# Two token roots by one product with a tile of ones and a power on 288 columns, and a final stage in two token halves: a decoder step on one core

## The chip, the core and the metric

The kernel runs on one core of a Trainium2 chip. The metric is the device time of one execution in microseconds. TensorE (PE in the profile) does the matrix products, VectorE (DVE) and ScalarE (ACT) the elementwise work, GpSimd (POOL) a few small operations, SyncE (SP) issues nearly all transfers.

## The reference

One step of a decoder with a single layer, in f32, for 256 prompt tokens and 8 x 4 sample tokens: 288 columns in all, 2048 features. Each of the nine sequences has its own conditioning vector, and so its own shift, scale and gate.

```python
def _rms(x, gain):
    y = xf * lax.rsqrt(jnp.mean(xf * xf, axis=-1, keepdims=True) + EPS)
    return y * gain

h = _rms(x, g_mix) * (1 + sc_m) + sh_m
proj = h @ w_in                       # seven parts, 9216 columns
...                                   # short convolution, gated MLP mixer, merge
x = x + gt_m * (merged @ w_out)
h2 = _rms(x, g_ffn) * (1 + sc_f) + sh_f
gate, up = jnp.split(h2 @ w_ffn_in, 2, axis=-1)
x = x + gt_f * ((silu(gate) * up) @ w_ffn_out)
y = _rms(x, g_final)
```

There are four means of squares: of x before `w_in` (the first root), of v inside the mixer, of x before `w_ffn_in` (the second root), and of the final x. Each gives one number for each token, mean to the power of -0.5, with which all features of that token are multiplied.

## The kernel before, in words

Features lie on the partitions, in 16 tiles of 128, and the 288 tokens on the columns. Every weight tile is loaded as f32 (`raw`) and split into a high part by a cast on ScalarE (L458) and a low part by a subtraction on VectorE (L464, in the first stage L249); the activations are split too. `triple` (L230, L233, L235) makes three products for each tile: high by high, high by low, low by high. The conditioning products (L401) are placed between the blocks.

TensorE's order is written out by hand: a list of steps, in which `later(f, gap)` puts a small piece of work behind so many further triples. In the first stage, up to `free`, the order of ScalarE, VectorE and SyncE is the program's order too; there `jobs` are run one at a time when a finished tile has been evicted. Afterwards a scheduler orders these engines. On each engine instructions run in their order, so one that waits holds up those behind it.

A root is made in four moves. The squares are summed over the 16 tiles on VectorE (`acc`, in the first stage `q`). `square_sum` (L204) takes 128 tokens at a time as weights and multiplies with one column of `ones`, which leaves the sums with the tokens on the partitions, 128 x 3. `roots` makes mean plus epsilon on VectorE (L217) and the power on GpSimd (L218), with a tile of -0.5 as exponent. `rstd_bcast` (L225) spreads the three columns back over all partitions by three transpositions.

First root: `sums1` and `norm1` are put behind 12 and 8 triples in the block `wA[2]`. `norm1` copies the result to `rb` on ScalarE (L622); `normed` (L309) multiplies x with it, and from there h1 is made (low parts in L657), which `wA[4]` needs. Before that the products run on x that is not yet normed (`xe`), and are put right later.

Second root: `rstd2` puts the sums 9 triples into the block `fk[0]`, the transpositions (`norm2`) 7 triples later, the copy is L931. The four blocks `fk` run on x without the norm (`xg`); the blocks `fi` behind them need h2 = `normed` (L309), scaled and shifted (L318, L321, L322) and split (L323, L328).

The final stage: the last residual (L345 for the prompt tokens, L351 and L354 for the sample tokens), its square (L173), the sums, one root for all tokens, and `finish` multiplies x by the spread root in nine pieces of one or two feature tiles (L986), each stored at once (L987). `warm` (L581) runs idle products in the waits.

Of the kernel before, what the change touches and what calls it, by code (L numbers as in the profile page):

```python
# [24 lines left out]
RAW = 7  # L25
# [6 lines left out]
EPS = 1e-6  # L32
# [21 lines left out]
TB = (0, 128, 160)  # L54
# [47 lines left out]
def _body(tc, nc, d, pc, pw, pslot, ptmp, pps):  # L102
    ids = [0]

    def nm(s):
        ids[0] += 1
        return f"{s}_{ids[0]}"

    def const(name, shape, dt=F32):
        return pc.tile(shape, dt, tag=name, name=name)  # L110

    def slot(dt=F32, shape=(P, T)):
        return pslot.tile(list(shape), dt, tag="s", name=nm("s"), padded_shape=[P, TU])
# [28 lines left out]
    x = const("x", [P, 16, T])  # L142
# [5 lines left out]
    ones = const("ones", [P, P])  # L148
    V.memset(ones, 1.0)
    mhalf = const("mhalf", [P, 16])  # L150
# [7 lines left out]
    mod = const("mod", [P, 96, NC])  # L158
# [7 lines left out]
    class SquareSum:  # L166
        def __init__(self):
            self.acc, self.last = None, None

        def add(self, a, cuts=((0, T),)):  # L170
            q = tmp() if self.last is not None else ptmp.tile([P, T], F32, tag="acc", name=nm("acc"), bufs=1)
            for o, e in cuts:
                A.activation(q[:, o:e], a[:, o:e], AF.Square)  # L173
            if self.last is not None:
                if self.acc is None:
                    self.acc = self.last
                else:
                    V.tensor_tensor(self.acc, self.acc, self.last, ALU.add)  # L178
            self.last = q

    def token_rstd(ss, n, half=False, gaps=None):
        got = {}
        V.tensor_tensor(ss.acc, ss.acc, ss.last, ALU.add)

        def fold():
            got["ps"] = psmisc()
            square_sum(got["ps"], ss.acc, True, True)

        steps = [fold, lambda: roots(got, n, half)]
        for f, gap in zip(steps, gaps or (0, 0, 0)):  # L190
            if gaps:
                later(f, gap)
            else:
                f()
        return got

    def sums(got, ss, first):
        if first:
            got["ps"] = psmisc()
        square_sum(got["ps"], ss.acc if first else ss.last, first, not first)  # L200

    def square_sum(ps, a, first, last):
        for tb, o in enumerate(TB):
            PE.matmul(  # L204
                ps[:, tb : tb + 1],
                a[:, o : o + 128],
                ones[:, 0:1],
                start=first and tb == 0,
                stop=last,
                skip_group_check=True,  # L210
            )

    def roots(got, n, half):
        ps = got["ps"]
        r = got["r"] = ptmp.tile([P, 3], F32, tag="r", name=nm("r"), bufs=2)
        e = ptmp.tile([P, 3], F32, tag="e", name=nm("e"), bufs=2)
        V.tensor_scalar(e, ps[:, 0:3], 1.0 / n, EPS, ALU.mult, ALU.add)  # L217
        G.tensor_tensor(r, e, mhalf[:, 0:3], ALU.pow)  # L218
        if half:
            V.tensor_scalar(r, r, 0.5, None, ALU.mult)  # L220

    def rstd_bcast(got):
        r, ps = got["r"], psmisc()
        for tb, o in enumerate(TB):
            PE.transpose(ps[:, o : o + P], r[:, tb : tb + 1].to_broadcast([P, P]), ident)  # L225
        return ps[:, :T]

    def triple(out, w, a, first, last, turn=False):
        (wh, wl), (ah, al) = w, a
# [46 lines left out]
    def later(f, gap=0):  # L276
        if not pending:
            since[0] = 0
        pending.append((f, gap))
# [27 lines left out]
    def normed(kt, rb):  # L307
        t = slot()
        V.tensor_tensor(t, x[:, kt, :], rb, ALU.mult)  # L309
        return t  # L310
# [27 lines left out]
            if i >= 2:  # L338
                finish_(ks[i - 2])

    def residual(m, ps, gt0, prompt_first=False):
        t = tmp()

        def prompt():
            V.scalar_tensor_tensor(  # L345
                x[:, m, :TP], ps[:, :TP], mod[:, gt0 + m, 0:1], x[:, m, :TP], ALU.mult, ALU.add
            )

        if prompt_first:
            prompt()  # L350
        V.tensor_tensor(sam(t[:, TP:]), sam(ps[:, TP:T]), bc4(mod[:, gt0 + m, 1:]), ALU.mult)  # L351
        if not prompt_first:
            prompt()
        V.tensor_tensor(x[:, m, TP:], t[:, TP:], x[:, m, TP:], ALU.add)  # L354

    def gelu2(a):
# [8 lines left out]
    class Step:  # L365
        defer = False
        raw = None
        parts = None

    class Ada(Step):  # L370
# [17 lines left out]
        half = None  # L388
# [183 lines left out]
    S = {}  # L572
# [5 lines left out]
    def warm(n, out=None):  # L578
        out = idle if out is None else out
        for _ in range(n):  # L580
            PE.matmul(out[:, :T], wb[:, :P], wb, start=True, stop=True)  # L581
# [30 lines left out]
        }  # L612

    def sums1():
        got = S["r1"] = {"ps": psmisc()}
        square_sum(got["ps"], S.pop("sq"), True, True)
        roots(got, D, False)

    def norm1():
        ps = rstd_bcast(S["r1"])  # L620
        S["rb1"] = ptmp.tile([P, T], F32, tag="rb", name=nm("rb"), bufs=1)
        A.copy(S["rb1"], ps)  # L622

        make_h1(0, 2)

    made = {}
# [144 lines left out]
    def sinkD(m, ps):  # L771
        a = part[m]
        V.tensor_tensor(a, ps[:, :T], a, ALU.add)  # L773
        if 32 <= m < 40:
            gelu2(a)
            if m == 32:
                S["accv"] = SquareSum()
            S["accv"].add(a)
        elif 24 <= m < 32:
            gelu2(a)  # L780
            u2[m - 24] = a
        elif m >= 40:
            A.activation(a, a, AF.Tanh, scale=0.5)
        elif m >= 16:
            mix_conv(m - 16)
# [22 lines left out]
            SY.dma_start(d["o_z"], zout)  # L808

    def v_stats():  # L810
        S["rv"] = token_rstd(S["accv"], 4096, True, (2, 0))
# [111 lines left out]
    h2, xg = {}, {}  # L923

    def rstd2():
        S["r2"] = token_rstd(S["acc2"], D, gaps=(9, 0))

    def norm2():
        ps = rstd_bcast(S["r2"])
        S["rb2"] = ptmp.tile([P, T], F32, tag="rb", name=nm("rb"), bufs=1)  # L930
        A.copy(S["rb2"], ps)  # L931
# [30 lines left out]

    def sink_fo(q):
        def f(m, ps):
            ending = q == 3 and m == 15
            residual(m, ps, 80, ending)
            if q == 3:
                if m == 0:
                    S["acc3"] = SquareSum()
                S["acc3"].add(x[:, m, :], ((0, TP), (TP, T)) if ending else ((0, T),))  # L970
                A.activation(x[:, m, :], x[:, m, :], AF.Copy, scale=gfin[:, m : m + 1])

        return f

    def finish():
        got, acc, keep = {}, S["acc3"], psmain()
        sums(got, acc, True)
        warm(5, keep)
        sums(got, acc, False)
        warm(10, keep)  # L980
        roots(got, D, False)
        rb = rstd_bcast(got)
        cuts = (0, 1, 2, 4, 6, 8, 10, 12, 14, 16)
        for i, j in zip(cuts, cuts[1:]):
            v = x[:, i:j, :]
            V.tensor_tensor(v, v, rb.unsqueeze(1).to_broadcast([P, j - i, T]), ALU.mult)  # L986
            SY.dma_start(d["o_y"][:, i:j, :], v)  # L987


    rh1 = h1.__getitem__  # L990
# [28 lines left out]
    steps = [Do(lambda: warm(24)), a0[0], Do(lambda: warm(5)), a0[1]]  # L1019
# [50 lines left out]
    n = len(steps)  # L1070
# [30 lines left out]
    for s in steps:  # L1101
# [11 lines left out]
        i = pos[id(s)]  # L1113
# [119 lines left out]
```

## Time and profile before

| | |
|---|---|
| median of 3 runs | 1627.19 us (1626.94 to 1627.59) |
| the profiled execution | 1627.47 us |
| its span | 1625.7 us |
| TensorE products, weight loads | 1614.2, 1550.0 us busy |
| VectorE, ScalarE, GpSimd | 1016.5, 736.1, 20.8 us busy |
| moved by transfers | 357.60 MB |

The span is the profiled time from the first instruction to the last; the rest of the execution's time lies around it. In a row of the timeline stand start, duration, engine, line, operation, what is written and read, and in brackets the engine's idle time before and what ended it. Rows of several instructions have one start and their whole duration. The chain of work that ended last is followed back from the last instruction; its rows have start, length, engine, tile and line.

### The profile page before, as it was taken

What the parts mean: (1) busy time and instruction counts of PE and PEld (TensorE: products, weight loads), DVE (VectorE), ACT (ScalarE), POOL (GpSimd) and SP (SyncE); (2) the same over time, 40 slices, a digit from 0 to 9 for tenths busy, and PEclk for the clock granted to TensorE, in tenths of its full rate; (3) what the DMA queues carried; (4) which work ended last, traced back from release to release, by engine and by line L of the source; (5) the groups of instructions that cost most, each with busy time, mean ns of one, the idle gap of its engine ahead of it and who ended that gap; (6) DMA issues with size and microseconds to landing.
All of it is one profiled execution on the core that took longest, in us unless ns stands there. A gap on an engine that the chain in (4) does not pass through costs nothing.

```text
span 1625.7 us, 31608 instructions
## 1 busy us (share of the span) xinstructions
PE 1614.2 (99%) x12649; PEld 1550.0 (95%) x12649; DVE 1016.5 (63%) x2196; ACT 736.1 (45%) x1357; POOL 20.8 (1%) x65
## 2 busy tenths in 40 slices
PE   9999999999999999999999999999999999999997
PEld 8998999999999999999999999999999999999997
DVE  6676788877755567667744555555555555555565
ACT  5633344643444334456633444444444444344453
POOL 0000000000000000011000000000000000000000
PEclk9999999999999999999999999999999999999999
DMA  9887866777777666654576556453464534644341
GB/s 374 325 319 276 318 232 212 281 275 295 294 296 310 260 258 225 245 175 160 186 303 263 210 179 207 157 173 110 169 222 156 175 114 161 225 159 171 113 156 59
DMA packets 59428, 357.60 MB, mean 220 GB/s; under 512 B 6768, under 2 KB 9872, under 8 KB 28560
## 3 DMA queue, kind: packets, MB, share of 16 engines
q1 hardware_dynamic: 58992, 355.45, 59.8%
q8 instruction: 99, 1.62, 0.4%
q14 instruction: 49, 0.40, 0.1%
q10 hardware_dynamic: 288, 0.13, 0.0%
HBM read 352.46 MB, written 3.09 MB: 219 GB/s over the span
## 4 chain that ended last, share of the span: by engine, by line
PE 98%; DMA 1%; DVE 0%; issue 0%; SPq 0%; DVEq 0%; ACT 0%
PE pm L230 31%; PE pm L233 30%; PE pm L235 30%; PE ada L401 5%; DMA raw<-in_a 1%; DVE x L986 0%; PE px L204 0%; PE px L233 0%; PE px L230 0%; PE px L825 0%; PE px L235 0%; PE px L866 0%; PE pm L581 0%; PE px L867 0%; PE px L868 0%; PE px L225 0%
## 5 line engine op out<-in xcount | busy, mean ns | idle before, releaser
L230 PE MATMUL pm<-s,hi 128*128 128x288 f32 (+1 forms) x3750 | 1109.0, 296 | 0.0
L233 PE MATMUL pm<-s,hi 128*128 128x288 f32 (+1 forms) x3750 | 1105.0, 295 | 0.0
L235 PE MATMUL pm<-s,lo 128*128 128x288 f32 (+1 forms) x3738 | 1101.2, 295 | 0.0
L458 ACT CAST hi<-raw 128x512 fp32r<-128x512 f32 (+1 forms) x963 | 587.2, 612 | 809.3 <-PE pm L233 780.1
L464 DVE TENSOR_TENSOR lo<-raw,hi 128x512 fp32r<-128x512 f32 (+1 forms) x849 | 577.6, 682 | 438.8 <-ACT hi L458 426.3
L230 PEld LDWEIGHTS pm<-s,hi 128*128 128x128 f32 x3750 | 705.1, 188 | 15.2 <-issue 13.3
L233 PEld LDWEIGHTS pm<-s,hi 128*128 128x128 f32 x3750 | 704.7, 188 | 0.0
L235 PEld LDWEIGHTS pm<-s,lo 128*128 128x128 f32 x3738 | 702.7, 188 | 0.0
L249 DVE TENSOR_TENSOR lo<-raw,hi 128x512 fp32r<-128x512 f32 x111 | 74.6, 675 | 28.9 <-ACT hi L458 28.2
L401 PE MATMUL ada<-raw,cs 128*32 128x512 f32 (+2 forms) x1152 | 88.2, 452 | 0.7 <-DMA raw<-in_a 0.6
L401 PEld LDWEIGHTS ada<-raw,cs 128*32 128x32 f32 x1152 | 30.8, 110 | 45.7 <-issue 41.4
L773 DVE TENSOR_TENSOR s<-pm,s 128x288 f32<-128x288 f32 x72 | 32.8, 456 | 19.8 <-PE pm L235 19.8
L345 DVE SCALAR_TENSOR_TENSOR x<-pm,mod,x 128x256 f32<-128x256 f32 x80 | 38.0, 475 | 2.7 <-PE pm L235 2.7
L304 DVE TENSOR_TENSOR s<-t,s 128x288 fp32r<-128x288 f32 (+1 forms) x76 | 34.5, 458 | 6.4 <-ACT s L302 6.4
L302 ACT CAST s<-t 128x288 fp32r<-128x288 f32 (+1 forms) x76 | 32.5, 432 | 12.9 <-DVE t L805 12.4
L951 DVE SCALAR_TENSOR_TENSOR t<-t,pm 128x288 f32<-128x288 f32 x42 | 19.1, 454 | 20.6 <-PE pm L235 20.6
L765 DVE TENSOR_TENSOR s<-pm,s 128x288 f32<-128x288 f32 x48 | 21.8, 454 | 10.6 <-PE pm L235 9.5
L351 DVE TENSOR_TENSOR t<-pm,mod 128x32 f32<-128x32 f32 x80 | 15.3, 191 | 18.5 <-PE pm L235 18.5
L750 DVE SCALAR_TENSOR_TENSOR s<-pm,s 128x256 f32<-128x256 f32 x48 | 23.0, 480 | 4.1 <-PE pm L235 4.1
L173 ACT ACTIVATE t<-x 128x288 f32<-128x288 f32 (+2 forms) x31 | 13.5, 437 | 20.6 <-DVE x L354 17.4
L756 DVE TENSOR_TENSOR s<-s,rb 128x288 f32<-128x288 f32 x48 | 21.5, 447 | 0.0
L178 DVE TENSOR_TENSOR acc<-acc,t 128x288 f32<-128x288 f32 x34 | 15.5, 455 | 8.7 <-ACT t L173 8.7
(141 smaller groups left out, 476.2 us busy)
## 6 DMA issues: line engine op xcount, KB each, us to landing
raw<-in_fi SPq DMA_DIRECT2D x84, 1024.0 KB, 4.8
raw<-in_a SPq DMA_DIRECT2D x64, 1024.0 KB, 9.3
raw<-in_f SPq DMA_DIRECT2D x64, 704.0 KB, 4.0
raw<-in_wD SPq DMA_DIRECT2D x34, 1024.0 KB, 5.5
raw<-in_aE SPq DMA_DIRECT2D x16, 1024.0 KB, 9.7
raw<-in_wo SPq DMA_DIRECT2D x16, 1024.0 KB, 6.5
raw<-in_wC SPq DMA_DIRECT2D x19, 768.0 KB, 4.4
raw<-in_pa SPq DMA_DIRECT2D x8, 1024.0 KB, 6.0
```

The source lines that it names most:

```text
L230: PE.matmul(out, wh, ah, start=first, stop=False)
L233: end_ = PE.matmul(out, wh, al, start=False, stop=turn and last)
L235: end_ = PE.matmul(out, wl, ah, start=False, stop=last)
L249: lows.pop(0)[1]()
L302: A.copy(hi, a)
L304: V.tensor_tensor(lo, a, hi.bitcast(F32), ALU.subtract)
L345: V.scalar_tensor_tensor(x[:, m, :TP], ps[:, :TP], mod[:, gt0 + m, 0:1], x[:, m, :TP], ALU.mult, ALU.add)
L401: PE.matmul(acc[32 * j : 32 * j + 32, :w], cs[:, kt, :], self.raw[:, o : o + w], start=kt == 0, stop=kt == 15, tile_position=(0, 32 * j), ...
L458: A.copy(hi, self.raw[:, s * 128 : e * 128])
L464: sub()
L750: V.scalar_tensor_tensor(t[:, :TP], ps[:, :TP], t[:, T : T + 1], t[:, :TP], ALU.add, ALU.add)
L773: V.tensor_tensor(a, ps[:, :T], a, ALU.add)
```

## The change

At the first and the second root `spread_root` takes the place of sums, power, transpositions and copy. One f32 product has the whole tile of ones as weights and the summed squares, 288 columns, as the moving side. All partitions get the sums of all tokens at once. The mean on VectorE and the power on GpSimd then run on 128 x 288 instead of 128 x 3, and the result is `rb` itself. `norm1` no longer has an instruction of TensorE; the step `norm2` is gone, so that the making of h2 follows the root in the list.

The root of v keeps the old way. In the final stage the last tile has its own code: residual and square in pieces of 128, 128 and 32 tokens, all engines in the program's order. Two halves, tokens 0 to 127 and 128 to 287, each have their own sums, mean, power (128 x 1 and 128 x 2) and transpositions (one and two). The products go to tiles of the weight pool instead of x, four for the first half and three for the second, into two outputs.

```diff
+    def spread_root(a):
+        ps, e = psmisc(), tmp()
+        rb = ptmp.tile([P, T], F32, tag="rb", name=nm("rb"), bufs=1)
+        PE.matmul(ps[:, :T], ones, a, start=True, stop=True)
+        V.tensor_scalar(e, ps[:, :T], 1.0 / D, EPS, ALU.mult, ALU.add)
+        G.tensor_tensor(rb, e, mhalf[:, 0:1].to_broadcast([P, T]), ALU.pow)
+        return rb
...
     def sums1():
-        got = S["r1"] = {"ps": psmisc()}
-        square_sum(got["ps"], S.pop("sq"), True, True)
-        roots(got, D, False)
+        S["rb1"] = spread_root(S.pop("sq"))
 
     def norm1():
-        ps = rstd_bcast(S["r1"])
-        S["rb1"] = ptmp.tile([P, T], F32, tag="rb", name=nm("rb"), bufs=1)
-        A.copy(S["rb1"], ps)
-
         make_h1(0, 2)
...
     def rstd2():
-        S["r2"] = token_rstd(S["acc2"], D, gaps=(9, 0))
+        acc = S["acc2"]
+        V.tensor_tensor(acc.acc, acc.acc, acc.last, ALU.add)
+
+        def spread():
+            S["rb2"] = spread_root(acc.acc)
+
+        later(spread, 9)
...
-    steps += [fk[0], Do(norm2, 7), mk_h2(0, 6), fk[1], mk_h2(6, 11), fk[2], mk_h2(11, 16), fk[3]]
+    steps += [fk[0], mk_h2(0, 6), fk[1], mk_h2(6, 11), fk[2], mk_h2(11, 16), fk[3]]
...
     def finish():
-        got, acc, keep = {}, S["acc3"], psmain()
-        sums(got, acc, True)
-        warm(5, keep)
-        sums(got, acc, False)
-        warm(10, keep)
-        roots(got, D, False)
-        rb = rstd_bcast(got)
...
+        summed(0, acc, True)
+        summed(1, acc, True)
+        warm(3, keep)
+        summed(0, q, False)
+        ra = rooted(0)
+        warm(1, keep)
+        summed(1, q, False)
+        rb = rooted(1)
+        warm(4, keep)
+        spread(0, ra)
+        warm(3, keep)
+        spread(1, rb)
+        stored(0, (0, 2, 5, 10, 16))
+        stored(1, (0, 4, 10, 16))
```

TensorE at the second root, before, in `fk[0]`: the sums, and seven triples further on the transpositions.

```order
5241 L235 MATMUL px_9653<-s_9069,lo_9554 128x298
5242 L204 MATMUL px_9684<-ones,acc_8378 128x1 x3
5243 L230 MATMUL pm_9654<-s_9069,hi_9552 128x298
...
5263 L235 MATMUL pm_9656<-s_9078,lo_9558 128x298
5264 L225 MATMUL px_9713<-cp,r_9688 128x128 x3
5265 L230 MATMUL px_9653<-s_9161,hi_9637 128x298
```

The same place now (`acc` holds the summed squares; lines are those of the changed kernel).

```order
5239 L220 MATMUL px_9645<-s_9063,hi_9544 128x298
5240 L222 MATMUL px_9645<-s_9061,lo_9546 128x298
5241 L210 MATMUL px_9676<-acc_8370,ones 128x288
5242 L217 MATMUL pm_9646<-s_9061,hi_9544 128x298
5243 L220 MATMUL pm_9646<-s_9063,hi_9544 128x298
```

One product stands where the sums stood, and the transpositions have no successor.

VectorE at the second root, before: the mean (L217), the low parts of the weights of `fk[1]` (L464), and the first readers of the root (L309).

```order
1227 L464 TENSOR_TENSOR lo_9643<-raw_9082,hi_9641 128x512
1228 L217 TENSOR_SCALAR e_9689<-px_9684 128x3
1229 L464 TENSOR_TENSOR lo_9647<-raw_9082,hi_9645 128x512
1230 L464 TENSOR_TENSOR lo_9651<-raw_9082,hi_9649 128x512
1231 L309 TENSOR_TENSOR s_9719<-x,rb_9717 128x288
1232 L309 TENSOR_TENSOR s_9721<-x,rb_9717 128x288
```

And now, with the mean as L211, the low parts as L444 and the readers as L296.

```order
1227 L444 TENSOR_TENSOR lo_9635<-raw_9074,hi_9633 128x512
1228 L211 TENSOR_SCALAR t_9677<-px_9676 128x288
1229 L444 TENSOR_TENSOR lo_9639<-raw_9074,hi_9637 128x512
1230 L296 TENSOR_TENSOR s_9703<-x,rb_9678 128x288
1231 L296 TENSOR_TENSOR s_9705<-x,rb_9678 128x288
1232 L308 TENSOR_TENSOR t_9707<-s_9703,gm_90 128x32
1233 L309 TENSOR_TENSOR t_9707<-t_9707,mod 128x32
1234 L308 TENSOR_TENSOR t_9715<-s_9705,gm_90 128x32
1235 L444 TENSOR_TENSOR lo_9643<-raw_9074,hi_9641 128x512
```

The last low part of `fk[1]` now stands behind the first readers of the root.

More of the change, by code (lines that the diff above doesn't have):

```diff
@@ L168, in __init__, with add @@
             self.acc, self.last = None, None
-        def add(self, a, cuts=((0, T),)):
+        def add(self, a):
             q = tmp() if self.last is not None else ptmp.tile([P, T], F32, tag="acc", name=nm("acc"), bufs=1)
-            for o, e in cuts:
-                A.activation(q[:, o:e], a[:, o:e], AF.Square)
+            A.activation(q, a, AF.Square)
             if self.last is not None:
@@ L179, in add, with token_rstd @@
             self.last = q
-    def token_rstd(ss, n, half=False, gaps=None):
+    def token_rstd(ss, n):
         got = {}
@@ L186, in fold @@
             got["ps"] = psmisc()
[L187 to L194, printed above, removed]
-        return got
[L197 to L226, printed above, removed]
+            for tb, o in enumerate(TB):
+                PE.matmul(
+                    got["ps"][:, tb : tb + 1],
+                    ss.acc[:, o : o + 128],
+                    ones[:, 0:1],
+                    start=tb == 0,
+                    stop=True,
+                    skip_group_check=True,
+                )
@@ new lines, in roots @@
+        def roots():
+            r = got["r"] = ptmp.tile([P, 3], F32, tag="r", name=nm("r"), bufs=2)
+            e = ptmp.tile([P, 3], F32, tag="e", name=nm("e"), bufs=2)
+            V.tensor_scalar(e, got["ps"][:, 0:3], 1.0 / n, EPS, ALU.mult, ALU.add)
+            G.tensor_tensor(r, e, mhalf[:, 0:3], ALU.pow)
+            V.tensor_scalar(r, r, 0.5, None, ALU.mult)
+        later(fold, 2)
+        later(roots, 0)
+        return got
+    def spread_root(a):
[5 more added lines that the diff above has]
+        return rb
@@ L339, in modulate, with residual @@
                 finish_(ks[i - 2])
-    def residual(m, ps, gt0, prompt_first=False):
+    def residual(m, ps, gt0):
         t = tmp()
[L344 to L350, printed above, removed]
         V.tensor_tensor(sam(t[:, TP:]), sam(ps[:, TP:T]), bc4(mod[:, gt0 + m, 1:]), ALU.mult)
-        if not prompt_first:
-            prompt()
+        V.scalar_tensor_tensor(
+            x[:, m, :TP], ps[:, :TP], mod[:, gt0 + m, 0:1], x[:, m, :TP], ALU.mult, ALU.add
+        )
         V.tensor_tensor(x[:, m, TP:], t[:, TP:], x[:, m, TP:], ALU.add)
@@ L964, in f @@
         def f(m, ps):
-            ending = q == 3 and m == 15
-            residual(m, ps, 80, ending)
+            if q == 3 and m == 15:
+                return last_tile(ps)
+            residual(m, ps, 80)
             if q == 3:
@@ L969, in f @@
                     S["acc3"] = SquareSum()
-                S["acc3"].add(x[:, m, :], ((0, TP), (TP, T)) if ending else ((0, T),))
+                S["acc3"].add(x[:, m, :])
                 A.activation(x[:, m, :], x[:, m, :], AF.Copy, scale=gfin[:, m : m + 1])
         return f
-    def finish():
-        got, acc, keep = {}, S["acc3"], psmain()
-        sums(got, acc, True)
-        warm(5, keep)
-        sums(got, acc, False)
-        warm(10, keep)
-        roots(got, D, False)
-        rb = rstd_bcast(got)
[L983 to L987, printed above, removed]
+    tail = contextlib.ExitStack()
@@ new lines, in last_tile, with prompt @@
+    def last_tile(ps):
+        acc, xl, q, t = S["acc3"], x[:, 15, :], tmp(), tmp()
+        V.tensor_tensor(acc.acc, acc.acc, acc.last, ALU.add)
+        tail.enter_context(tc.manual_schedule(engines={A.engine, V.engine, G.engine, SY.engine}))
+        S["q"] = q
+        def prompt(o, e):
+            V.scalar_tensor_tensor(xl[:, o:e], ps[:, o:e], mod[:, 95, 0:1], xl[:, o:e], ALU.mult, ALU.add)
+            A.activation(q[:, o:e], xl[:, o:e], AF.Square)
+        prompt(0, P)
+        prompt(P, TP)
+        V.tensor_tensor(sam(t[:, TP:]), sam(ps[:, TP:T]), bc4(mod[:, 95, 1:]), ALU.mult)
+        V.tensor_tensor(xl[:, TP:], t[:, TP:], xl[:, TP:], ALU.add)
+        A.activation(q[:, TP:], xl[:, TP:], AF.Square)
+        A.activation(xl, xl, AF.Copy, scale=gfin[:, 15:16])
@@ new lines, in finish, with summed, rooted, spread @@
+    def finish():
+        acc, q, keep = S["acc3"].acc, S["q"], psmain()
+        halves = ((0,), (1, 2))
+        pss, rbs = [psmisc(), psmisc()], [psmisc(), psmain()]
+        def summed(i, a, first):
+            for n, tb in enumerate(halves[i]):
+                PE.matmul(
+                    pss[i][:, n : n + 1],
+                    a[:, TB[tb] : TB[tb] + P],
+                    ones[:, 0:1],
+                    start=first and n == 0,
+                    stop=not first,
+                    skip_group_check=True,
+                )
+        def rooted(i):
+            n = len(halves[i])
+            r = ptmp.tile([P, 3], F32, tag="r", name=nm("r"), bufs=2)
+            e = ptmp.tile([P, 3], F32, tag="e", name=nm("e"), bufs=2)
+            V.tensor_scalar(e[:, :n], pss[i][:, :n], 1.0 / D, EPS, ALU.mult, ALU.add)
+            G.tensor_tensor(r[:, :n], e[:, :n], mhalf[:, :n], ALU.pow)
+            return r
+        def spread(i, r):
+            for n, tb in enumerate(halves[i]):
+                o = TB[tb] - TB[halves[i][0]]
+                PE.transpose(rbs[i][:, o : o + P], r[:, n : n + 1].to_broadcast([P, P]), ident)
+        def stored(i, cuts):
+            w, name = ((P, "o_ya"), (T - P, "o_yb"))[i]
+            t0 = TB[halves[i][0]]
+            for o, e in zip(cuts, cuts[1:]):
+                st = pw.tile([P, (e - o) * w], F32, tag="raw", name=nm("st"), bufs=RAW, padded_shape=[P, 2048])
+                v = st.rearrange("p (m t) -> p m t", t=w)
+                V.tensor_tensor(
+                    v, x[:, o:e, t0 : t0 + w], rbs[i][:, :w].unsqueeze(1).to_broadcast([P, e - o, w]), ALU.mult
+                )
+                SY.dma_start(d[name][:, o:e, :], v)
+        summed(0, acc, True)
[12 more added lines that the diff above has]
+        stored(1, (0, 4, 10, 16))
+        tail.close()
@@ L1221 @@
     res = _run(nc, [{f"in_{k}": v for k, v in arr.items()}], core_ids=[0]).results[0]
-    y = res["o_y"].reshape(P, 16, T).transpose(2, 1, 0).reshape(T, D)
+    y = np.concatenate([res["o_ya"].reshape(P, 16, P), res["o_yb"].reshape(P, 16, T - P)], 2)
+    y = y.transpose(2, 1, 0).reshape(T, D)
     z = res["o_z"].reshape(P, 8, 18).transpose(2, 1, 0).reshape(18, 1024)
```

8 lines of the change are left out of this document (2 added, 6 removed).

## The prediction

> **What bounds the kernel now.** I read the page's head and its chain first, then the groups of GpSimd (POOL), then the timeline around the three places that the change touches.
>
> ```profile
> span 1625.7 us, 31608 instructions
> PE 1614.2 (99%) x12649; PEld 1550.0 (95%) x12649; DVE 1016.5 (63%) x2196; ACT 736.1 (45%) x1357; POOL 20.8 (1%) x65
> PE 98%; DMA 1%; DVE 0%; issue 0%; SPq 0%; DVEq 0%; ACT 0%
> ```
>
> TensorE's products set the end almost alone: 98% of the chain, and 1614.2 of 1625.7 us busy. So only three things can move the time: TensorE work taken off, a TensorE wait put in, or the last 13 us, where TensorE has finished. The change does some of each.
>
> The chain in order of time prices the TensorE work of a root.
>
> ```profile
> 43.42 0.67 PE px L204 x6
> 44.09 0.24 PE pm L230
> 49.15 0.33 PE px L225 x3
> 552.40 0.22 PE px L866 x2
> 761.90 0.56 PE px L204 x6
> 762.47 0.25 PE pm L230
> ```
>
> At the second root the three products with a column of ones take 0.56 us, the product behind them 0.25 instead of some 0.14 (0.11 lost), the three transpositions 0.33 (row of the first root): 1.0 us.
>
> The timeline says how soon the result is needed, at the second root (VectorE is DVE, PE is TensorE).
>
> ```profile
> 761.74 0.73 PE L204 MATMUL px<-ones,acc 128*128 128x1 f32 x6
> 763.27 0.15 DVE L217 TENSOR_SCALAR e<-px 128x3 f32<-128x3 f32 x1
> 764.37 0.69 DVE L464 TENSOR_TENSOR lo<-raw,hi 128x512 fp32r<-128x512 f32 x1 [0.94 <-ACT hi L458]
> 766.62 0.82 DVE L309 TENSOR_TENSOR s<-x,rb 128x288 f32<-128x288 f32 x2
> 790.16 0.82 DVE L328 TENSOR_TENSOR s<-t,s 128x288 fp32r<-128x288 f32 x2
> 791.57 0.30 PE L233 MATMUL pm<-s,hi 128*128 128x288 f32 x1
> ```
>
> L309 is the first reader of the root, L328 makes the last low part of h2 (ready at 790.98), and TensorE takes that at 791.57. In between VectorE has no room.
>
> ```profile
> 766.62:772.00 5.38, 5.38 (x41) 5.38 (x41) 5.09 (x21) 4.90 (x12) 0.00 (x0) 1.00 0.61 198
> 772.00:778.00 6.00, 6.00 (x46) 6.00 (x45) 6.00 (x20) 5.18 (x12) 0.00 (x0) 1.00 0.34 106
> 784.00:791.00 7.00, 7.00 (x55) 7.00 (x54) 6.96 (x23) 6.57 (x17) 0.00 (x0) 1.00 0.54 197
> ```
>
> Behind the length of each stretch stand the busy times of TensorE's products, its weight loads, VectorE, ScalarE and GpSimd. VectorE's is 5.09 of 5.38 us, then 6.00 of 6.00, at the end 6.96 of 7.00. Its slack over the stretch is 0.59 us at the end and 0.33 us of idle time: about 0.9 us. A root that comes later than that shifts the end of h2, and TensorE waits as long.
>
> The first root has more room.
>
> ```profile
> 44.13 0.16 DVE L217 TENSOR_SCALAR e<-px 128x3 f32<-128x3 f32 x1
> 44.21 0.68 DVE L249 TENSOR_TENSOR lo<-raw,hi 128x512 fp32r<-128x512 f32 x1
> 49.19 0.47 DVE L744 COPY s<-pm 128x298 f32<-128x298 f32 x1 [2.09 <-PE pm L235]
> 50.31 0.45 DVE L309 TENSOR_TENSOR s<-x,rb 128x288 f32<-128x288 f32 x1
> 54.53 0.45 DVE L657 TENSOR_TENSOR s<-t,s 128x288 fp32r<-128x288 f32 x1
> 57.10 0.29 PE L233 MATMUL pm<-s,hi 128*128 128x288 f32 x1
> ```
>
> VectorE first uses the root at 50.31, the second low part of h1 is ready at 54.98, TensorE takes it at 57.10: 2.1 us of slack.
>
> **The change part by part.** *TensorE at the roots.* Each root's 1.0 us goes, and one f32 product on 288 columns comes. L866, f32 on 128 columns, is two records and 0.22 us; by columns 0.22 x 288/128 = 0.50 us, with the same 0.11 us behind it 0.6. Saved: 0.4 us at the second root, 0.5 at the first (there the three products take 0.67 instead of 0.56, row at 43.42): 0.9 us.
>
> *VectorE and ScalarE at the roots.* The mean on 288 columns of PSUM costs about what L744 does, 0.47 instead of 0.16 us. It hides in VectorE's idle 2.09 us before L744, and in the 0.94 us before 764.37 at the second root. ScalarE's copy of the broadcast root goes, off the path. VectorE takes its next instructions in a fixed order, so behind a late root stand the low parts of the next weights (L464) and, at the first root, evictions; TensorE waits for both.
>
> *The power on GpSimd* is the open price. These are its rows, and those of VectorE's beside which they ran:
>
> ```profile
> 44.37 1.23 POOL L218 TENSOR_TENSOR r<-e,mhalf 128x3 f32<-128x3 f32 x1 [33.36 <-DVE e L217]
> 449.71 0.74 POOL L849 TENSOR_TENSOR s<-s,cp 128x256 f32<-128x256 f32 x1 [135.85 <-DMA s<-in_wsg]
> 716.20 0.24 POOL L918 TENSOR_TENSOR t<-x,gm 128x32 f32<-128x32 f32 x1 [6.90 <-DVE acc L178]
> 717.31 0.69 DVE L464 TENSOR_TENSOR lo<-raw,hi 128x512 fp32r<-128x512 f32 x1
> 717.34 0.77 POOL L918 TENSOR_TENSOR t<-x,gm 128x32 f32<-128x32 f32 x1 [0.73 <-DVE s L304]
> 763.51 0.85 POOL L218 TENSOR_TENSOR r<-e,mhalf 128x3 f32<-128x3 f32 x1 [3.43 <-DVE e L217]
> ```
>
> A multiplication takes 0.24 us on 32 columns and 0.74 on 256: 0.50/224 = 2.2 ns a column. If a power's columns cost as much and the rest of its 0.85 us is paid once, 288 columns take 0.85 + 285 x 0.0022 = 1.5 us: the lower bound. For the upper one I split the 0.85 us. The multiplication at 717.34 ran beside L464, which ended at 718.00, 0.66 us later, and lost 0.77 - 0.24 = 0.53 us: it had passed 0.13 us before it was held up. The power at 44.37 ran beside L249, which ended at 44.89, 0.52 us later, and lost 1.23 - 0.85 = 0.38: 0.14 us. Up to there the two operations cost the same. What is left is 0.11 us for 32 columns of a multiplication, and 0.71 us for three of a power: 0.24 us a column if all of it is work on columns, 288 x 0.24 + 0.13 = 69 us. With the multiplication's fixed part of 0.17 us (0.24 - 32 x 0.0022) and its slope taken off instead, (0.85 - 0.17)/3 = 0.227 us a column, and 0.17 + 288 x 0.227 = 65.5 us. I take 65.5: of all rows the three-column power is the nearest, and nothing in it but columns is seen to last. [...]
>
> *What it costs.* Second root: VectorE's mean ends near 763.7, the power starts at 763.9 and ends 65.5 us later at 829.4, instead of 766.62 for L309: 62.8 us late, less 0.9: TensorE waits 61.9 us. First root: the mean comes after L744 and ends near 44.6, the low part behind it may hold the power up for 0.5 us, so the root is there at 45.2 + 65.5 = 110.7 instead of 50.31: 60.4 us late, less 2.1: 58.3 us. The 0.9 us of TensorE saved is lost in these waits.
>
> *The final stage.* Now one mean, one power and three transpositions for all tokens, then nine products and stores:
>
> ```profile
> 1612.82 0.72 PE L204 MATMUL px<-ones,acc 128*128 128x1 f32 x6
> 1613.02 0.48 DVE L345 SCALAR_TENSOR_TENSOR x<-pm,mod,x 128x256 f32<-128x256 f32 x1 [2.73 <-PE pm L235]
> 1614.87 0.16 DVE L217 TENSOR_SCALAR e<-px 128x3 f32<-128x3 f32 x1 [1.05 <-PE px L204]
> 1616.02 0.54 PE L225 MATMUL px<-cp,r 128*128 128x128 f32 x3
> 1616.59 5.47 DVE L986 TENSOR_TENSOR x<-x,px 128x288 f32<-128x288 f32 x9 [1.56 <-PE px L225]
> 1617.08 5.35 SPq L987 DMA_DIRECT2D o_y<-x  x9
> 1621.00:1622.00 1.00, 0.00 (x0) 0.00 (x0) 1.00 (x2) 0.00 (x0) 0.00 (x0) 0.77 1.01 385
> 1622.00:1623.00 1.00, 0.00 (x0) 0.00 (x0) 0.06 (x1) 0.00 (x0) 0.00 (x0) 0.50 1.05 389
> ```
>
> The DMA engines are full (share 1.01 and 1.05, 385 to 389 GB/s), and the stores' bytes stay: 16 x 288 x 128 x 4 B = 2.36 MB, 6.1 us. So the gain is what the first store leaves earlier. For the first 128 tokens the residual has half its columns (0.2 us less of 0.48), one product instead of three (0.4 us less), one transposition instead of three (0.3 us less): 0.9 us. The second half's mean and power run beside the first half's stores; uncovered they would cost one power, 0.85 us. Bounds: nothing (seven larger stores instead of nine land later), and 1.6 us (all of VectorE's wait before L986). I take 0.9.
>
> *Sum.* 1625.7 + 61.9 + 58.3 - 0.9 = 1745.0 us of span; the profiled run took 1627.47 us, 1.8 more than its span (and 0.3 over the median of 1627.19): **1747 us**.
>
> **The rivals.** *The power is paid once* (not slower): at 1.5 us the root of the second place is there at 765.4, before 766.62, and the first at 46.7: no wait. The time is 1627.5 - 0.9 - 0.9 = 1625.7 us. It decides while the power stays under 3.6 us at the second root (767.5 - 763.9) and 7.2 us at the first (52.4 - 45.2). For it speaks that no row shows a second size; against it the 0.71 us behind the read, which 32 columns of a multiplication don't have.
>
> *The loop overlaps columns*: between the two, by their geometric mean, 9.9 us (33 ns a column). The waits are 9.9 - 3.6 = 6.3 and 9.9 - 7.2 = 2.7 us: 1627.5 + 9.0 - 0.9 = 1635.6 us. From a power of about 8 us on it is slower by over 0.2% (3.3 us, about what a measurement of this kernel can tell from no change). [...] No run here shows which loop the power has.
>
> *Everything hides and the tail gives more*: stores that leave 2.6 us earlier (VectorE's 1.56 us before L986 and 1.05 before the mean) and the 0.9 us make 1624.0 us, just 0.2% faster. The chain of residual, square, product and power stays, which speaks against it.
>
> **How the numbers follow.** Columns priced in full: 0.45, its own range 1720 to 1760. The low end has 0.18 us a column, a quarter less than 0.24 for a part paid once (52 us, 27 us less over both roots); the high end 0.24 (69 us, 8 us more), and 5 us for TensorE's clock: after its last work at 1616.6 the granted clock (the figure before the last two) fell to 0.77 and 0.50 within some 5 us, and if it takes as long to rise, each of two restarts loses half of that. Paid once: 0.34, 1625.7. Overlapped: 0.15, 1636. A larger tail: 0.06. The range has to hold the first two, so it reaches from 1624.5 to 1760, with overlap between them. Faster 0.06, same 0.34, slower 0.45 + 0.15 = 0.60.
>
> **What would show it.** The group of POOL powers on 288 columns: over 50 us each bears the forecast out, 1 to 3 us the first rival, near 10 the second. In the final stage one column should take 0.4 us and two 0.6 instead of 0.85; two equal rows near 0.85 would mean a fixed price. In the chain there should be two waits of TensorE, near 45 and 765 us, each ended by a low part or an eviction of VectorE, which itself waits for POOL. The root's product should last 0.5 us, and the first store leave 0.9 us earlier behind the last product. The forecast is wrong if VectorE's first reader of either root starts within 3 us of the mean.

## The result, and the profile after

The changed kernel takes **1710.64 us** (median of 5 runs, 1710.28 to 1712.19) against 1627.19 us of the kernel before (5 runs on the same chip, 1626.92 to 1627.60): a ratio of 1.0512, with 95% between 1.0501 and 1.0523. It is slower by 83 us. Its profiled run took 1710.71 us with a span of 1708.9.

First the head of its page, the chain's shares, and the group of the two large powers (busy time, mean of one in ns, idle time before and what ended it).

```profile
span 1708.9 us, 31567 instructions
PE 1616.3 (95%) x12631; PEld 1550.8 (91%) x12631; DVE 1017.9 (60%) x2196; ACT 735.9 (43%) x1356; POOL 111.9 (7%) x66
PE 91%; POOL 5%; DVE 2%; DMA 1%; ACT 1%; issue 0%; SPq 0%; DVEq 0%; ACTq 0%
L212 POOL TENSOR_TENSOR rb<-t,mhalf 128x288 f32<-128x288 f32 x2 | 92.8, 46416 | 37.7 <-DVE t L211 37.7
```

GpSimd went from 20.8 to 111.9 us of busy time and from nothing to 5% of the chain. TensorE's busy time grew by 2.1 us, though it has 18 instructions fewer: behind the two waits its products take longer, as the stretches below show. The same group in the timeline, with the two times apart:

```profile
44.76 46.61 POOL L212 TENSOR_TENSOR rb<-t,mhalf 128x288 f32<-128x288 f32 x1 [33.94 <-DVE t L211]
804.68 46.23 POOL L212 TENSOR_TENSOR rb<-t,mhalf 128x288 f32<-128x288 f32 x1 [3.73 <-DVE t L211]
```

And the other powers of this kernel by their shape, from the groups of GpSimd: three columns (the root of v), two and one (the halves of the final stage).

```profile
L200 POOL TENSOR_TENSOR r<-e,mhalf 128x3 f32<-128x3 f32 x1 | 1.1, 1059 | 262.6 <-DVE e L199 262.6
...
L991 POOL TENSOR_TENSOR r<-e,mhalf 128x2 f32<-128x2 f32 x1 | 0.7, 703 | 0.0
L991 POOL TENSOR_TENSOR r<-e,mhalf 128x1 f32<-128x1 f32 x1 | 0.5, 549 | 847.9 <-DVE e L990 847.9
```

One column takes 0.549 us, two take 0.703: 0.154 us a column and 0.395 us paid once. From the 0.85 us of three columns in the kernel before to the mean of 46.42 us there are 285 columns and 45.57 us: 0.160 us a column. (The 1.06 us of the root of v above don't fit that line: VectorE's L340, with two inputs, ran beside it. Beside the 0.85 us there was no such operation.)

Who waited for them: TensorE's and VectorE's waits (in total, times, longest).

```profile
PE px L222 <- DVE lo L444: 41.5, 1, 41.5
PE pm L217 <- DVE s L718: 39.1, 1, 39.1
```
```profile
DVE s L296 <- POOL rb L212: 86.1, 2, 45.0
```

VectorE stood 86.1 us at L296, the first reader of the root, and behind it in its fixed order stood an eviction (L718) at the first root and a low part of the weights (L444) at the second. TensorE waited for these two. What it did afterwards is in the stretches behind each wait; the columns are length, TensorE's products, weight loads, VectorE, ScalarE, GpSimd, then the granted clock.

```profile
92.00:94.00 2.00, 1.71 (x6) 1.49 (x6) 1.93 (x8) 2.00 (x5) 0.00 (x0) 0.50 0.03 8
94.00:96.00 2.00, 2.00 (x26) 1.19 (x28) 2.00 (x6) 1.28 (x4) 0.00 (x0) 0.50 0.00 0
96.00:98.00 2.00, 2.00 (x33) 1.39 (x25) 0.55 (x1) 0.00 (x0) 0.00 (x0) 0.85 0.61 169
98.00:104.00 6.00, 6.00 (x50) 5.83 (x52) 4.36 (x9) 3.27 (x8) 0.00 (x0) 1.00 0.85 323
...
854.00:856.00 2.00, 2.00 (x9) 1.98 (x9) 2.00 (x10) 2.00 (x5) 0.00 (x0) 0.50 0.70 270
856.00:858.00 2.00, 2.00 (x10) 2.00 (x10) 2.00 (x8) 2.00 (x6) 0.00 (x0) 0.56 0.49 201
858.00:860.00 2.00, 2.00 (x17) 2.00 (x16) 2.00 (x5) 1.46 (x4) 0.00 (x0) 1.00 0.00 0
```

For 4 to 5 us behind each wait the clock stands at half. The chain in order of time shows the price at the first root, and the end of the products (start, length, engine, tile, line):

```profile
93.65 0.25 PE pm L220
...
94.15 3.29 PE ada L381 x48
97.44 0.33 PE pm L217
...
1697.39 0.56 PE px L977 x6
```

And the same places before:

```profile
54.31 0.14 PE pm L235
54.45 2.09 PE ada L401 x48
56.53 0.33 PE pm L230
...
1612.98 0.56 PE px L204 x6
```

The product behind the conditioning products starts at 97.44 instead of 56.53: 40.9 us later. The first sums of the final stage, the mark for the end of the products, start 84.4 us later: 43.5 us came at the second root. In the first shift, six products at about 0.25 instead of 0.14 us and 3.29 instead of 2.09 us for the conditioning products are about 2 us.

At the second root the chain has another shape. Behind the power stand only VectorE and ScalarE for 25.8 us, and TensorE comes back at 876.71 (L296 reads the root, L315 makes the low parts of h2, L933 is an eviction):

```profile
850.94 0.83 DVE s L296 x2
...
875.10 0.74 DVE s L315 x2
875.83 0.74 DVE s L933 x2
...
876.71 0.37 PE pm L217
```

From L296 to L933 VectorE is busy 24.69 of 24.81 us; before, the same stretch was 23.94 of 24.27 us. So the second root shifts the program as far as the making of h2 comes late. TensorE's wait of 41.5 us and the 2 us that it then loses at half clock lie beside that row: when the row ends, TensorE is only 0.26 us ahead of it, the time that it waits in front of L217 at 876.71.

The final stage is shorter. Its stores, in the timeline:

```profile
1700.25 2.39 SPq L1008 DMA_DIRECT2D o_ya<-st  x4
1703.04 2.46 SPq L1008 DMA_DIRECT2D o_yb<-st  x3
```

The first one leaves 1700.25 - 1697.39 = 2.86 us behind that mark; in the kernel before it was 1617.08 - 1612.98 = 4.10 us. From the mark to the end of the span it is 11.5 us instead of 12.7. So the span grew by 40.9 + 43.5 - 1.2 = 83.2 us, which is 1708.9 - 1625.7.

### The profile page after: what moved, and what is told of

It is laid out like the page before. It is cut to its first block, busy times and chain, and to the rows that moved or that the text cites. A ratio compares the mean times of both kernels' runs of the same rounds, so it can differ in the third digit from the quotient of the medians.

```text
span 1708.9 us, 31567 instructions
## 1 busy us (share of the span) xinstructions
PE 1616.3 (95%) x12631; PEld 1550.8 (91%) x12631; DVE 1017.9 (60%) x2196; ACT 735.9 (43%) x1356; POOL 111.9 (7%) x66
## 4 chain that ended last, share of the span: by engine, by line
PE 91%; POOL 5%; DVE 2%; DMA 1%; ACT 1%; issue 0%; SPq 0%; DVEq 0%; ACTq 0%
PE pm L217 29%; PE pm L220 28%; PE pm L222 28%; POOL rb L212 5%; PE ada L381 5%; DMA raw<-in_a 1%; DVE lo L444 0%; DVE st L1005 0%; DVE s L315 0%; DVE s L296 0%; ACT hi L438 0%; PE px L799 0%; ACT s L310 0%; ACT t L305 0%; DVE q L577 0%
## 5 line engine op out<-in xcount | busy, mean ns | idle before, releaser
L217 PE MATMUL pm<-s,hi 128*128 128x288 f32 (+1 forms) x3750 | 1110.4, 296 | 39.3 <-DVE s L718 39.1
L444 DVE TENSOR_TENSOR lo<-raw,hi 128x512 fp32r<-128x512 f32 (+1 forms) x849 | 578.6, 683 | 436.5 <-ACT hi L438 423.9
L217 PEld LDWEIGHTS pm<-s,hi 128*128 128x128 f32 x3750 | 705.9, 188 | 55.0 <-DVE s L718 39.3
L212 POOL TENSOR_TENSOR rb<-t,mhalf 128x288 f32<-128x288 f32 x2 | 92.8, 46416 | 37.7 <-DVE t L211 37.7
L296 DVE TENSOR_TENSOR s<-x,rb 128x288 f32<-128x288 f32 x32 | 14.0, 452 | 86.1 <-POOL rb L212 86.1
L747 DVE TENSOR_TENSOR s<-pm,s 128x288 f32<-128x288 f32 x72 | 32.9, 457 | 19.8 <-PE pm L222 19.8
L222 PE MATMUL px<-s,lo 128*128 128x298 f32 x16 | 5.3, 331 | 41.5 <-DVE lo L444 41.5
L305 ACT ACTIVATE t<-s,mod,gm 128x256 f32<-128x256 f32 x24 | 13.9, 598 | 50.8 <-DVE s L296 46.4
```

The source lines that it names most:

```text
L212: G.tensor_tensor(rb, e, mhalf[:, 0:1].to_broadcast([P, T]), ALU.pow)
L217: PE.matmul(out, wh, ah, start=first, stop=False)
L222: end_ = PE.matmul(out, wl, ah, start=False, stop=last)
L444: sub()
```

## The experiments

The theory after the result: the power has a price for each column, 0.16 us, and both roots wait for it almost in full; the rest of the change gains a little. Rivals: the broadcast exponent makes the power slow, not its columns; or another part of the change (the wide product, the new order, the final stage) carries some of the 83 us. The kernels ran on several chips; the kernel before took 1627.19 to 1627.57 us on them, so between chips a difference of 0.4 us says nothing.

### The parts by themselves

The roots alone: `spread_root` in the kernel before, with its old final stage.

```diff
-        square_sum(got["ps"], S.pop("sq"), True, True)
-        roots(got, D, False)
+        S["rb1"] = spread_root(S.pop("sq"))
...
-        S["r2"] = token_rstd(S["acc2"], D, gaps=(9, 0))
+        later(spread, 9)
```

> Both new roots with the final stage of before. Theory: the two waits are untouched and only the final stage's 1.2 us is given back: 1710.6 + 1.2 = 1711.8 us. Rival (the final stage gains nothing): 1710.6 us.

Measured: 1711.42 us (1711.26 to 1711.66), ratio 1.0516 (1.0501 to 1.0530). That is 0.8 us above the changed kernel, between the two cases, and too little to tell them apart; the loss of 84 us is there without the new final stage.

The final stage alone: the changed kernel with both roots made the old way (the first root's lines; the second root's are those of the next edit).

```diff
-        S["rb1"] = spread_root(S.pop("sq"))
+        S["r1"] = token_root(S.pop("sq"))
...
+        S["rb1"] = rstd_bcast(S["r1"])
```

> Both roots as before (three columns of sums, power on 128x3, transpositions, copy), with the new final stage alone. Theory (the loss is the two wide powers; the final stage gains what its first store leaves earlier, 1.2 us in the profile of after): 1627.2 - 1.2 = 1626.0 us, no wait of TensorE near either root. Rival (the final stage's larger, fewer stores land later and eat the gain, or part of the loss lies in the final stage): 1627.2 us or more.

Measured: 1626.25 us (1626.00 to 1627.11, 11 runs), the kernel before on that chip 1627.55; ratio 0.9992 (0.9983 to 1.0001). It looks like 1.3 us of gain, which this interval doesn't quite separate from nothing.

One root new, the other old, with the new final stage. First the changed kernel with the second root the old way:

```diff
-            S["rb2"] = spread_root(acc.acc)
-
-        later(spread, 9)
+        S["r2"] = token_root(acc.acc, 9)
...
-    steps += [fk[0], mk_h2(0, 6), fk[1], mk_h2(6, 11), fk[2], mk_h2(11, 16), fk[3]]
+    steps += [fk[0], Do(norm2, 7), mk_h2(0, 6), fk[1], mk_h2(6, 11), fk[2], mk_h2(11, 16), fk[3]]
```

> The first root in the new way, the second in the old way, the new final stage. Theory (two independent waits): the first root shifted TensorE by 40.9 us in the profile of after (clock and product included), the final stage gives 1.2: 1627.2 + 40.9 - 1.2 = 1666.9 us. Rival (a wait at the first root makes room that shortens the second one's, or the other way round): over 2 us off this sum.

Measured: 1667.24 us, ratio 1.0243 (1.0229 to 1.0256). Then the first root the old way and the second new, by the edit of `sums1` and `norm1` shown above:

```diff
-        S["rb1"] = spread_root(S.pop("sq"))
+        S["r1"] = token_root(S.pop("sq"))
```

> The second root in the new way, the first in the old way, the new final stage. Theory: the second root shifted TensorE by 43.5 us in the profile of after: 1627.2 + 43.5 - 1.2 = 1669.5 us, 2.6 us more than with the first root alone, since VectorE has 0.9 us of slack there and 2.1 at the first. Rival: equal to the first root's price or less.

Measured: 1669.46 us, ratio 1.0257 (1.0243 to 1.0271). The waits of TensorE, in the kernel with the first root and in that with the second:

```profile
PE pm L250 <- DVE s L751: 39.1, 1, 39.1
```
```profile
PE px L255 <- DVE lo L477: 41.5, 1, 41.5
```

Each has its own wait and not the other. Over the final stage alone they cost 41.0 and 43.2 us, together 84.2; 1626.25 + 84.2 = 1710.5 against 1710.64 measured. The two roots add up, and all of the loss is theirs.

### The size of the power

Half of the columns go through the power:

```diff
-        G.tensor_tensor(rb, e, mhalf[:, 0:1].to_broadcast([P, T]), ALU.pow)
+        G.tensor_tensor(rb[:, : T // 2], e[:, : T // 2], mhalf[:, 0:1].to_broadcast([P, T // 2]), ALU.pow)
+        V.tensor_copy(rb[:, T // 2 :], e[:, T // 2 :])
```

> The changed kernel with the power on the first 144 columns alone; the other 144 columns of the root are the mean itself, without the power. Theory (the power costs 0.37 us and 0.16 us for each column): 23.4 us each, 23 less than the 46.4 measured, and TensorE's two waits of 39.1 and 41.5 us shrink by as much, to 16 and 18.5: 1710.6 - 46 = 1665 us. Rival (a price for a wide instruction as such, paid once for each call): the powers stay at 46 us and the time at 1711 us. Rival (work grows faster than the columns): below 20 us each, time under 1658 us.

Measured: 1665.49 us (1664.56 to 1666.39), ratio 1.0231 (1.0216 to 1.0247). TensorE's waits are 15.8 and 19.5 us, for the 16 and 18.5 expected. Three columns, by the same edit:

```diff
+        G.tensor_tensor(rb[:, :3], e[:, :3], mhalf[:, :3], ALU.pow)
+        V.tensor_copy(rb[:, 3:], e[:, 3:])
```

> The changed kernel with the power on 3 columns alone; the other 285 columns of the root are the mean itself, without the power. Theory: the powers take 0.85 us, no wait of TensorE is left at either root, and what remains are the gains: the product of 0.5 us instead of sums and transpositions (0.9 us over both) and the final stage (1.2 us): 1627.2 - 2.1 = 1625.1 us. Rival (the f32 product, the mean on 288 columns or the earlier place of the making of h2 cost as well): 1626.0 us, the final stage's gain alone, or more.

Measured: 1624.76 us (1624.49 to 1624.91, 11 runs), ratio 0.9983 (0.9974 to 0.9991). The groups of the powers, half and three columns:

```profile
L212 POOL TENSOR_TENSOR rb<-t,mhalf 128x144 f32<-128x144 f32 x2 | 46.7, 23354 | 37.5 <-DVE t L211 37.5
```
```profile
L212 POOL TENSOR_TENSOR rb<-t,mhalf 128x3 f32<-128x3 f32 x2 | 1.9, 972 | 37.7 <-DVE t L211 37.7
```

144 columns take 23.35 us, 288 take 46.42: 23.07/144 = 0.160 us for each of the second 144, as for the first. The five sizes measured, from one column to 288, lie close to a straight line. Both kernels leave the power out on the other columns, so their outputs are not those of the reference; VectorE's copy fills these columns instead. (It and a low part ran beside the power of three columns, which took 0.97 us here instead of the expected 0.85.) With three columns everything else of the change is there (the wide product, the mean on 288 columns, the missing step, the new final stage), and the time is 2.8 us under the kernel before on that chip, 1627.55. So the rest of the change, taken together, costs nothing, and the loss is the power's columns.

In that kernel TensorE doesn't wait at either root, and the chain shows the new product's price without a wait behind it, at both roots:

```profile
43.66 0.49 PE px L210 x2
44.15 0.13 PE pm L218
...
761.45 0.49 PE px L210 x2
761.94 0.14 PE pm L218
```

The exponent as a full tile of 128 x 288 instead of one column read 288 times:

```diff
+        m = tmp()
+        V.memset(m, -0.5)
-        G.tensor_tensor(rb, e, mhalf[:, 0:1].to_broadcast([P, T]), ALU.pow)
+        G.tensor_tensor(rb, e, m, ALU.pow)
```

> The changed kernel with the exponent read from a whole 128x288 tile of -0.5 (filled by VectorE ahead of each root) instead of one column repeated. Theory (the columns' work is the price): powers of 46 us as before, the time within 1 us of 1710.6. Rival (the repeated column makes the power slow): powers of a few us, 1626 to 1632 us.

Measured: 1711.77 us (1711.56 to 1712.06), ratio 1.0517 (1.0501 to 1.0533). The powers:

```profile
L214 POOL TENSOR_TENSOR rb<-t,t 128x288 f32<-128x288 f32 x2 | 93.1, 46528 | 38.8 <-DVE t L213 38.8
```

46.53 us instead of 46.42: the broadcast read isn't it. The time is 1.1 us above the changed kernel, a little more than the 1 us expected, and 80 us above the rival's.

### The clock behind the waits

The windows showed TensorE at half clock behind each wait. Is that a cost of standing idle? Idle products into the sums' tile, put in front of the instruction that waits (18 triples behind the first root's product, 19 behind the second's), should then win it back.

```diff
         since[0] += 1
+        fill = S.get("fill")
+        if fill:
+            fill[0] -= 1
+            if not fill[0]:
+                warm(fill[2], S.pop("fill")[1])
...
+        S["rb1"] = spread_root(S.pop("sq"), (18, 280))
...
+            S["rb2"] = spread_root(acc.acc, (19, 300))
```

> The change, with 280 and 300 idle products of TensorE put in front of the two places where it waits for the long power, some 35 and 38 us of the 39.1 and 41.5. The waits' causes stay. Theory: 2.3 and 2.1 us of the 83 lost are TensorE's clock, which stands at half for some 5 us behind each wait because TensorE stood idle; kept busy it starts at full clock, and the time is 1710.6 - 4.4 = 1706.2 us. Rival: behind the waits the products are slow because weights and evictions have to be caught up; then the time stays at 1710.6, or rises by what the idle products run over the wait.

Measured: 1722.39 us (1721.34 to 1724.26), ratio 1.0582 (1.0568 to 1.0597). Neither case came. The waits and two stretches behind the first one:

```profile
PE px L218 <- ACT hi L444: 9.1, 1, 9.1
PE pm L218 <- DVE s L724: 4.8, 1, 4.8
PE px L223 <- DVE lo L450: 4.7, 1, 4.7
```
```profile
92.00:94.00 2.00, 0.00 (x0) 0.00 (x0) 0.06 (x1) 0.00 (x0) 1.91 (x1) 0.64 0.00 0
94.00:96.00 2.00, 1.17 (x5) 1.17 (x6) 1.97 (x7) 1.56 (x4) 0.00 (x0) 0.50 0.00 0
```

The idle products took 0.123 us each and left waits of 4.8 and 4.7 us, and in these the clock fell to half. And a new wait of 9.1 us for a cast stands behind the second root. With the idle products in the program, the scheduler put 66 of VectorE's and 41 of ScalarE's instructions in other places, which the edit wasn't meant to do; that these places made the new wait is likely, not shown. So the next experiment leaves the second root alone and gives the first 310 products; VectorE's and ScalarE's orders are then those of the change.

```diff
-        S["rb1"] = spread_root(S.pop("sq"), (18, 280))
+        S["rb1"] = spread_root(S.pop("sq"), (18, 310))
```

> The change, with 310 idle products of TensorE in front of the first of the two places where it waits for the long power: at the 0.123 us that one took, 38.2 of the 39.1 us of wait, about 1 us left. VectorE's and ScalarE's orders are those of the change. Theory: behind this wait TensorE's products take 0.25 instead of 0.14 us for some 5 us, 2.3 us lost, only because the clock fell while TensorE stood idle; with 1 us of idle time the granted clock stays at 1.00, the products take 0.14 us from the first on, and the time is 1710.6 - 2.3 = 1708.3 us. Rival: what is slow there is not the clock; the first products take 0.25 us all the same, and the time stays at 1710.6 or above.

Measured: 1708.67 us (1708.28 to 1708.99), ratio 1.0498 (1.0480 to 1.0515). The stretches behind the first wait, and the products in the timeline:

```profile
90.00:92.00 2.00, 1.19 (x10) 0.70 (x8) 0.62 (x2) 0.12 (x1) 1.35 (x1) 1.00 0.00 0
92.00:94.00 2.00, 1.73 (x26) 1.42 (x30) 1.93 (x8) 2.00 (x5) 0.00 (x0) 1.00 0.00 0
```
```profile
92.27 0.41 PE L218 MATMUL pm<-s,hi 128*128 128x298 f32 x1 [1.09 <-DVE s L724]
92.52 0.30 PE L221 MATMUL pm<-s,hi 128*128 128x298 f32 x1
...
93.29 2.16 PE L387 MATMUL ada<-raw,cs 128*32 128x192 f32 x48
```

The first product starts when it did (92.27, in the change 92.29), but the clock stays at 1.00, products follow each other after 0.14 us, and the conditioning products begin at 93.29 instead of 94.15 and take 2.16 instead of 3.29 us: 0.9 + 1.1 = 2.0 us in the trace, 1.97 in the medians (2.3 expected). At the first root the half clock is a second price of the wait, some 2 us. At the second no run fills the wait cleanly, and the chain shown above speaks against such a price there: a TensorE that is 2 us faster behind that wait would stand longer in front of h2. The traces show 1.1 us of idle time that left the clock at 1.00, 4.8 us that halved it, and 4 to 5 us at half behind the waits. In the changed kernel the fall itself is seen: behind the last product in front of the first root's wait, which ends at 53.2, the clock is 0.81 in the stretch from 55 to 56 us and 0.50 from 56 on, so it fell some 2.4 us into the wait.

### Another way to the root

The form of the change can be kept if the power is not GpSimd's. ScalarE's square root and VectorE's reciprocal on 288 columns:

```diff
-        G.tensor_tensor(rb, e, mhalf[:, 0:1].to_broadcast([P, T]), ALU.pow)
+        A.activation(e, e, AF.Sqrt)
+        V.reciprocal(rb, e)
```

> The changed kernel with the root made by a square root on ScalarE and a reciprocal on VectorE, both on 128x288, instead of the power on GpSimd. Theory (a root that comes within 3.6 us of its mean at the second place and 7.2 at the first costs nothing): both waits vanish and the gains of product and final stage remain, 1625.1 us, the fastest of all. Rival (ScalarE, 4.90 of 5.38 us busy behind the second root, loses its place in the row by the square root and whatever goes with it, and h2 comes late): 1627 to 1632 us.

Measured: 1628.36 us (1627.53 to 1632.55, 11 runs), ratio 1.0008 (0.9999 to 1.0017). The rival's time held. Ahead of the second root the profiled run of this kernel is 0.9 us earlier than that with three columns (the same low part at 760.35 and 761.23), at the first sums of the final stage 2.8 us later (1614.34 and 1611.53): it loses 3.7 us behind the second root. One stretch there, in this kernel and in that with three columns, and the two new operations:

```profile
786.00:794.00 8.00, 6.02 (x38) 4.89 (x37) 7.87 (x29) 6.48 (x14) 0.00 (x0) 1.00 0.38 132
```
```profile
786.00:794.00 8.00, 8.00 (x62) 8.00 (x62) 7.86 (x24) 5.54 (x14) 0.00 (x0) 1.00 0.38 131
```
```profile
L213 DVE RECIPROCAL rb<-t 128x288 f32<-128x288 f32 x2 | 3.9, 1954 | 2.4 <-ACT t L212 2.4
```
```profile
43.52 1.28 ACT L212 ACT_TABLE_LOAD   x1
44.81 0.44 ACT L212 ACTIVATE t<-t 128x288 f32<-128x288 f32 x1
```

In the stretch TensorE makes 38 products in 8 us instead of 62, 24 x 0.134 = 3.2 us. The second root is ready 4.2 us behind its mean (762.39 to 766.55), more than the 3.6 us of the theory's own condition; and the reciprocal takes 1.95 us of VectorE, which has 0.9 us to spare there until TensorE needs the end of h2. From 764.6 to 788.7 us the chain holds VectorE's and ScalarE's work alone, and TensorE then waits four times for VectorE, 2.0 us in all. So h2 comes late, as the rival said; how much of it is VectorE's reciprocal and how much ScalarE's load and square root (1.28 + 0.44 us), no run separates. The load of ScalarE's function table takes 1.28 us; the activation starts 0.01 us behind it.

At the first root the reciprocal should fit. So the last kernel makes only that one with square root and reciprocal, the second root the old way, with the new final stage.

```diff
+        A.activation(e, e, AF.Sqrt)
+        V.reciprocal(rb, e)
...
+        S["r2"] = token_root(acc.acc, 9)
```

> The first root by the product with the tile of ones, with ScalarE's square root and VectorE's reciprocal on 288 columns in place of GpSimd's power; the second root the old way; the new final stage. Theory: the 1.95 us of the reciprocal fit in the first root's slack of 2.1 us and VectorE's idle time there, not in the second's 0.9; so the square root costs nothing here, TensorE's 0.5 us at the first root is kept, and the time is 1625.6 us (the new final stage alone: 1626.25; three columns at both roots: 1624.76). Rival: the two loads of a function table, 1.28 us each on ScalarE, hold up the casts that TensorE needs; then 1627 us or more.

Measured: 1625.74 us (1625.20 to 1626.13, 11 runs), the kernel before on that chip 1627.57; ratio 0.9988 (0.9979 to 0.9997). The theory's 1625.6 held, though the old way at both roots, 1626.25, lies just 0.5 us from it. This version is under both kernels: 85 us under the changed one, and some 2 us, hardly more than can be told, under the one before. In its timeline the reciprocal ends 2.5 us ahead of the first reader of the root.

```profile
45.73 1.95 DVE L246 RECIPROCAL rb<-t 128x288 f32<-128x288 f32 x1 [1.17 <-ACT t L245]
...
50.17 0.45 DVE L330 TENSOR_TENSOR s<-x,rb 128x288 f32<-128x288 f32 x1
```

## Why the prediction was right, and which term was off

The side, the mechanism and the places were right, and the time lies in the stated range, on the slower side, 36 us under the forecast of 1747. That range says little: it reached down to 1624.5 so as to hold the first rival too. The range of the favoured case alone, 1720 to 1760, misses 1710.6 by 9 us, and the powers, at 46 us, fall short of the "over 50 us each" that was to bear it out. Point by point:

- **The power priced by columns** was right in kind, and its size is the term that was wrong: 46.61 and 46.23 us instead of 65.5, 38.2 us less over both roots. The step that failed is the fixed part. The prediction took the multiplication's 0.17 us for it and laid the remaining 0.68 us of the three-column power on the columns, 0.227 us each. Measured are 0.40 us fixed and 0.154 to 0.160 us a column; even the low end's 0.18 us, meant to allow for a larger fixed part, was too much. One row of one size can't separate the two; the final stage of the changed kernel, with 0.549 and 0.703 us, does.
- **The upper and lower bound** (69 and 1.5 us) held the value.
- **The waits.** The places (near 45 and 765 us plus the shift of the first root) and the chain from GpSimd over VectorE's first reader to an eviction and a low part are borne out. With the measured powers, the prediction's own working gives shifts of 45.2 + 46.6 - 50.31 - 2.1 = 39.4 us and 763.9 + 46.2 - 766.62 - 0.9 = 42.6 us; measured are 40.9 and 43.5. At the first root, 40.9 is 38.9 and 2 us of clock. The slack of 2.1 us there was that of h1's end, while the wait ended with the eviction (the reader came 91.40 - 50.31 = 41.1 us late, TensorE waited 39.1); that the two slacks agree is luck. At the second root the slack was taken at the right place, the end of h2; the 0.9 us more are in part the low part of `fk[1]` (0.6 us), which now stands behind the first readers and lengthens VectorE's row, and which the working left out.
- **The clock** stood only at the high end of the range, with up to 5 us for two restarts. About 2 us at the first root belonged in the forecast, shown there by filling the wait. At the second root the clock falls as well, but by the trace it adds next to nothing, since VectorE's row sets the shift; no run tests that.
- **TensorE's saving at the roots**, 0.5 and 0.4 us: the new product takes 0.49 us and the one behind it 0.13, not 0.25, so it is 0.67 + 0.11 + 0.33 - 0.49 = 0.6 us and 0.56 + 0.11 + 0.33 - 0.49 = 0.5. As forecast, it is lost where the roots wait; in the kernel with three columns, 1.5 us under the final stage alone, it shows (1.1 us of the 1.5).
- **The final stage**: 1.2 us instead of 0.9 for the first store and for the end. The halves' powers take 0.549 and 0.703 us, not the 0.4 and 0.6 of the forecast, and not twice 0.85.
- **The rivals.** Paid once: refuted by 23.35 us for half the columns; its time of 1625.7 is about what the kernel with three columns takes (1624.76). Overlapping columns: refuted with its 33 ns a column and 9.9 us; a column costs 160 ns, the second 144 as much as the first. A larger tail: the final stage alone gives 1.3 us in the medians, 1.2 in the profile, not 2.6 or more.

The sum by the forecast's terms: 1747.0 - 38.2 = 1708.8 us with the power at its size; 1.5 us more at the first root, 0.9 more at the second and 0.3 less for the final stage make 1710.9, against 1710.7 in the profiled run.

## What to carry to other kernels

Take the price of an operation from two sizes before you change its size a hundredfold: with one row, what is paid once and what is paid for each column can't be told apart. Do a costly function where its values stand on the partitions (three columns) and spread the result afterwards; spreading first made it do 96 times the columns for the same 288 numbers. And a long wait of TensorE can cost more than its length: the clock fell to 0.50 in the wait of 39.1 us at the first root, and that cost some 2 us behind it. When the wait can't go, count the half-clock stretch behind it where TensorE is the next on the chain, as at the first root; where another engine's row has to be made up first, as at the second, it is hidden.

## What the runs showed of the hardware

- A power on GpSimd with f32 on 128 partitions takes 0.40 us and 0.16 us for each column, close to a straight line over 1, 2, 3, 144 and 288 columns (0.549, 0.703, 0.85, 23.35 and 46.42 us); that its exponent is one column read again and again changes nothing (46.42 against 46.53 us).
- VectorE's operations that read two tiles cost a power running beside them a fraction of a microsecond, not a part of its length: the long power took 46.61 us with three of them in its first 6 us and 46.23 with one, the power of three columns 1.23 us beside one and 0.85 without. These are single rows.
- In a wait of 4.8 us without products TensorE's granted clock fell to half (0.64 in the stretch from 92 to 94 us, 0.50 from 94 to 96), in one of 1.1 us it did not (1.00); behind the changed kernel's waits of 39.1 and 41.5 us it stood at half for 4.3 and 4.9 us.
- A reciprocal on VectorE takes 1.95 us for 128 x 288 f32, over four times a multiplication's 0.45.
